# The last product of the down projection ended in two halves of its tokens, and residual sums made by accumulating transfers

## The chip, the core and the metric

The kernel runs on one core of one Trainium2 chip. The metric is the device time of one execution in microseconds (us); the figure for a kernel is the median of its runs. One execution of the kernel was recorded by the hardware profiler, instruction by instruction. The engines are named as in the profile: PE multiplies matrices, PEld is its loading of weights, DVE and ACT work element by element, POOL and SP here mostly issue transfers (DMAs). Tiles are 128 partitions high; matmul results go to PSUM banks of 128 x 512 floats, everything else lies in SBUF.

## What is computed

One layer of a decoder trunk, 1024 tokens of width 1024 in float32: a token-mixing part (an RWKV-7 branch and an S5 branch, merged) and then a channel part, each with a norm before and after and a residual sum:

```python
        mixed = (g_rwkv * o_rwkv + g_s5 * o_s5) @ w_out[l]
        x = x + rms_norm(mixed, norm_mix_post[l])
        h = rms_norm(x, norm_ffn_pre[l])
        f = conv_ffn(h, ffn_w_up[l], ffn_conv_w[l], ffn_conv_b[l], ffn_w_down[l])
        x = x + rms_norm(f, norm_ffn_post[l])

def conv_ffn(h, w_up, conv_w, conv_b, w_down):
    L = h.shape[1]
    z = h @ w_up
    zp = jnp.pad(z, ((0, 0), (CONV_WIDTH - 1, 0), (0, 0)))
    z = conv_b + sum(conv_w[j] * zp[:, j:j + L] for j in range(CONV_WIDTH))
    gate, val = jnp.split(z, 2, axis=-1)
    return (jax.nn.gelu(gate) * val) @ w_down
```

`rms_norm` divides each token by the root of the mean of its squares over the 1024 channels and scales each channel by a gain. The change is in the last two lines of the layer: the product with `w_down` (2816 by 1024), its norm, and the residual sum that is the output.

## The kernel before

Channels lie on partitions and tokens along the free dimension, so the layer's output is eight blocks of 128 channels by 1024 tokens. Every float32 matmul is done as three: an operand is split into a rounded high part (ACT, line 227) and the rest (DVE, line 228), and high x high, high x low and low x high are summed.

Four stages follow each other: the mixing part, its output projection with the norms between the two parts (`mid_norms`), the up stage (`fast_up`), and the down stage (`down`). `mid_norms` calls `post_norm`, which stores the residual stream x after the mixing part to a DRAM array `X1`, one block of 128 channels and 512 tokens at a time.

**The up stage** makes, for each of 22 tiles of the hidden width, a value and a gate, convolves both over the tokens in tiles `y` (one activation at line 1356, two DVE steps at line 1358 each), applies Gelu to the gate (line 1290), multiplies (line 1291) and has POOL store the result to the DRAM array `ACT[i]` (line 1292). Its tiles lie in four pools, one above the other in each partition: `upz` (bytes 25920 to 46400), `ups` (to 66880), `upr` (the weights as they arrive, `r`, and one split tile; to 83264) and `upy` (three buffers for `y`; to 95552).

**The down stage** multiplies two-by-two blocks of the product in seven block products instead of eight, by sums and differences of blocks; each covers 11 tiles of 128 of the hidden width. The products run in the order p1, p2, p5, p6, p7, p4, p3. Each takes its 11 tiles in six groups (`DGROUPS`: two, two, one, two, two, two tiles). For a group, `operands` splits both sides into `wh`, `wl`, `xh`, `xl`, in a ring of three sets; `step` issues three matmuls of 512 columns (lines 1511 to 1513) for one tile and one of four output banks `d`. In the first and the last group the banks are done one after the other, in the others the tiles are. `p1` loads a group's A and T tiles, which stay in SBUF, and its right operand into a ring of four staging tiles `st`, and takes the difference of T and `st` on DVE (line 1466). Its pools on the lower side are `dqa` (S, B and `sq` tiles; bytes 25920 to 66880), `dqs` (the `st` ring; 66880 to 83264) and `dqb` (B tiles; to 95552): they lie where the up stage's pools lay.

The norm and the output of the first 512 tokens are done between the groups of p3 (`middle`): after group 0 the squares are summed over the channels by matmuls with a column of ones (line 246) and DVE makes the reciprocal root (`rstd`, lines 266 and 136 to 141, a chain of 12 small instructions); after group 1 matmuls with the identity spread it over the partitions (`spread`, line 272); after group 3 `outputs` makes eight blocks on DVE, each a product with gain and root (line 1555) and a sum with the residual (line 1463), which SP stores to the output. The residual blocks were loaded from `X1` by `resid`, into freed T tiles. The other 512 tokens go the same way after p3's last group, their residual loaded into freed A tiles: `c12` adds each finished bank to its partial sum and ACT squares it (line 1537).

The order of work on each engine is made by a scheduler from the order in which the kernel is written, priorities and estimated times, and each queue runs strictly in its order. A tile in a pool that lies over an earlier pool may be written only when the users of the earlier pool are done.

Of the kernel before, what the change touches and what calls it, by code (L numbers as in the profile page):

```python
# [18 lines left out]
D = 1024  # L19
# [52 lines left out]
class Kern:  # L72
# [169 lines left out]

    def sumsq(self, ss, sq, first):

        for tb in range(4):
            self.nc.tensor.matmul(ss[:, tb:tb + 1], sq[:, tb * 128:(tb + 1) * 128], self.ones1,
                                  start=first and tb == 0, stop=True, skip_group_check=True)
# [14 lines left out]

    def rstd(self, ss, eps, scale):

        v = self.small.tile([128, 4], F32, tag="rv", name=self.nm("rv"), bufs=2)
        self.nc.vector.tensor_scalar(v, ss[:, :4], scale, eps, ALU.mult, ALU.add)
        return self.rsqrt(v, 4, "nr")

    def spread(self, bc, y):

        for tb in range(4):
            self.nc.tensor.matmul(bc[:, tb * 128:(tb + 1) * 128], y[:, tb:tb + 1].to_broadcast([128, 128]),
                                  self.cst("ident"), start=tb == 0, stop=True, skip_group_check=True)
# [950 lines left out]
    def mid_norms(self, th, mx):  # L1224
# [7 lines left out]
        yield from self.post_norm(mx, s0, th, "g_mix_post", lambda k, o: self.a["x"][k * 128:k * 128 + 128, o],  # L1232
                                  lambda k, o: self.X1[k * 128:k * 128 + 128, o], squares=ss)
        y = self.rstd(ss, 1e-6, 1.0 / D)
# [180 lines left out]
    def down(self, dq0, dqf, dqt, dqa, dqs, dqb):  # L1415
# [91 lines left out]

        def step(op, q, m, ps, start, stop):
            (wh, wl), (xh, xl) = op
            c, x = slice(q * 512 + m * 128, q * 512 + m * 128 + 128), slice(q * 512, q * 512 + 512)  # L1510
            mm(ps, wh[:, c], xh[:, x], start=start, stop=False, skip_group_check=True)  # L1511
            mm(ps, wh[:, c], xl[:, x], start=False, stop=False, skip_group_check=True)  # L1512
            mm(ps, wl[:, c], xh[:, x], start=False, stop=stop, skip_group_check=True)  # L1513
# [3 lines left out]

        def product(prep, ps, first, evict, between=lambda g: None):

            for g in range(ng):  # L1520
# [20 lines left out]

        def resid(th):
            xs = []
            for m in range(0, NK, 2):
                t = cache("T" if th == 0 else "A", (0, 1, 3, 4)[m // 2])
                for q in range(2):
                    x = t[:, q * 512:q * 512 + 512]
                    nc.sync.dma_start(x, self.X1[(m + q) * 128:(m + q) * 128 + 128, th * 512:th * 512 + 512])
                    xs.append(x)
            return xs  # L1550

        def outputs(th, src, bc, xs):
            for m in OUTORD[th]:
                y = stage(0)[:, 0:512]
                V.scalar_tensor_tensor(y, src[m], self.vec("g_ffn_post", m), bc, ALU.mult, ALU.mult)
                add(y, y, xs[m])
                nc.sync.dma_start(self.out[m * 128:m * 128 + 128, th * 512:th * 512 + 512], y)
        acc = [None, None]
# [25 lines left out]

        def c12(m):
            add(f[1][m], f[1][m], x[m])
            if m < 3:
                squares(1, f[1][m])
            else:
                last.append(acc[1])  # L1590
                acc[1] = None
                squares(1, f[1][m])

        def middle(g):
            if g == 0:
                ss = bank(0)
                self.sumsq(ss, acc[0], True)
                d["y"] = self.rstd(ss, 1e-6, 1.0 / D)
                d["xs"] = resid(0)
            elif g == 1:  # L1600
# [3 lines left out]
                A.copy(d["bc"], bc)  # L1604
            elif g == 3:
                outputs(0, f[0], d["bc"], d["xs"])
                d["xs1"] = resid(1)
        d, last = {}, []
        product(p1, b, True, keep1)
# [4 lines left out]
        product(p4, b, False, c21)  # L1614
        product(p3, x, False, c12, middle)
        ss = bank(2)
        self.sumsq(ss, last[0], True)
        self.sumsq(ss, acc[1], False)
        y = self.rstd(ss, 1e-6, 1.0 / D)
        bc = bank(3)  # L1620
        self.spread(bc, y)
        outputs(1, f[1], bc, d["xs1"])

    def build(self):
        tc, nc = self.tc, self.nc
        with tc.tile_pool(name="const", bufs=1) as self.const, tc.tile_pool(name="small", bufs=1) as self.small, \
# [10 lines left out]
            self.YR = [dr(f"YR{m}") for m in range(4)]  # L1637
            self.X1 = dr("X1", (D, T))
            self.H0 = [dr(f"H0{k}", (128, 512)) for k in range(NK)]
# [174 lines left out]
DGROUPS = ((0, 1), (2, 3), (10,), (4, 5), (6, 7), (8, 9))  # L1814
OUTORD = ((0, 1, 2, 3, 4, 5, 6, 7), (4, 5, 6, 7, 0, 1, 2, 3))
NT2C = 7
# [73 lines left out]
```

## Time and profile before

| | us |
|---|---|
| median of 3 runs | 1600.54 |
| lowest and highest run | 1599.51, 1603.78 |
| the profiled execution, as timed | 1601.3 |
| its span, first to last instruction | 1599.5 |
| PE busy within the span | 1501.5 (94%) |
| DVE busy | 1130.4 (71%) |
| ACT busy | 694.0 (43%) |
| POOL busy | 154.9 (10%) |

A row of the timeline gives the start from the span's beginning, the length, the engine, the line of the kernel, the operation, the tiles written and read, the shape and the count of rows merged; in brackets stand the idle time of the engine before it and what ended that. SPq is the issue of a transfer on SP's queue. A row of groups gives the count, the busy time, the mean in ns of one instruction and the idle time before them. A row of windows gives a stretch, its length, the busy time of PE, PEld, DVE, ACT and POOL with their instructions, the clock granted to PE as a share, the share of the DMA engines' time in use and GB/s. A row of DMA issues gives the tiles, the queue, the count, the size of one and the median time from issue to landing.

### The profile page before, as it was taken

The numbers are of one execution on the slowest core, as the hardware profiler recorded it, in microseconds if no ns is written. First come the engines' busy times: TensorE is split into PE (matmuls) and PEld (weight loads), VectorE is DVE, ScalarE is ACT, GpSimd is POOL, SyncE is SP. The second block draws the span as 40 slices with busy tenths as digits, with TensorE's granted clock in tenths as the row PEclk, the third lists the DMA queues.
The fourth block names the chain that finished last, engine by engine and source line by source line (L and its number), as shares of the span: only waits on it lengthen the run. The fifth ranks groups of instructions, "written<-read, shape, count | busy, mean of one in ns | idle before, by whom it ended". The sixth has DMA issues, their size and how long they took to land.

```text
span 1599.5 us, 26116 instructions
## 1 busy us (share of the span) xinstructions
PE 1501.5 (94%) x10028; PEld 1203.0 (75%) x10028; DVE 1130.4 (71%) x2039; ACT 694.0 (43%) x1107; POOL 154.9 (10%) x226
## 2 busy tenths in 40 slices
PE   5999899899999989979997999999999999999995
PEld 4788788687666766657776888788888887878784
DVE  6798774655365557874667679877777777688777
ACT  5354442224333345454533545544544445443451
POOL 2100000414123142010000000000000000000000
PEclk9999999999998989989988999999999999999997
DMA  6164244343352364652484453322222225953722
GB/s 205 40 198 142 72 128 138 104 129 120 101 151 84 104 192 119 180 146 68 152 259 142 145 191 130 122 91 79 79 80 92 80 79 166 325 186 116 226 80 105
DMA packets 133420, 213.84 MB, mean 134 GB/s; under 512 B 38656, under 2 KB 44800, under 8 KB 133296
## 3 DMA queue, kind: packets, MB, share of 16 engines
q1 hardware_dynamic: 124208, 188.32, 36.2%
q0 software_dynamic: 7936, 21.77, 4.6%
q10 hardware_dynamic: 1152, 2.10, 0.3%
q8 instruction: 78, 1.28, 0.3%
q14 instruction: 46, 0.38, 0.1%
HBM read 156.56 MB, written 53.48 MB: 131 GB/s over the span
## 4 chain that ended last, share of the span: by engine, by line
PE 57%; DVE 8%; DMA 3%; issue 1%; ACT 1%; POOL 0%; SPq 0%; DVEq 0%; ACTq 0%
PE gm L173 4%; PE rp L1337 4%; PE rp L1339 4%; PE rp L1338 4%; PE d L1512 4%; PE d L1511 4%; PE d L1513 4%; PE gm L174 3%; PE gm L175 3%; PE ch L173 2%; PE mm L1338 2%; PE mm L1337 2%; PE mm L1339 2%; PE ch L174 2%; PE ch L175 2%; PE mm L173 2%
## 5 line engine op out<-in xcount | busy, mean ns | idle before, releaser
L173 PE MATMUL gm<-hh,wh 128*128 128x512 f32 x688 | 297.3, 432 | 7.3 <-ACT hh L227 2.1
L174 PE MATMUL gm<-hl,wh 128*128 128x512 f32 x688 | 275.1, 400 | 0.4 <-DVE hl L228 0.4
L175 PE MATMUL gm<-hh,wl 128*128 128x512 f32 x656 | 261.4, 398 | 0.0
L157 ACT CAST wh<-wf 128x512 fp32r<-128x512 f32 x179 | 110.9, 619 | 219.7 <-PE gm L174 133.5
L158 DVE TENSOR_TENSOR wl<-wf,wh 128x512 fp32r<-128x512 f32 x175 | 121.9, 697 | 103.4 <-ACT wh L157 83.1
L173 PEld LDWEIGHTS gm<-hh,wh 128*128 128x128 f32 x688 | 132.5, 193 | 46.0 <-issue 5.1
L174 PEld LDWEIGHTS gm<-hl,wh 128*128 128x128 f32 x688 | 132.8, 193 | 24.3 <-issue 1.9
L175 PEld LDWEIGHTS gm<-hh,wl 128*128 128x128 f32 x656 | 126.2, 192 | 28.6
L1511 PE MATMUL d<-xh,wh 128*128 128x512 f32 x308 | 121.6, 395 | 2.8 <-ACT xh L227 2.1
L1512 PE MATMUL d<-xl,wh 128*128 128x512 f32 x308 | 121.5, 394 | 2.9 <-DVE xl L228 2.9
L1513 PE MATMUL d<-xh,wl 128*128 128x512 f32 x308 | 121.1, 393 | 0.0
L1337 PE MATMUL rp<-t,h 128*128 128x512 f32 x216 | 84.4, 391 | 2.1 <-ACT p L1351 2.1
L1339 PE MATMUL rp<-t,l 128*128 128x512 f32 x216 | 84.2, 390 | 0.5 <-DVE l L228 0.5
L1338 PE MATMUL rp<-t,h 128*128 128x512 f32 x216 | 84.1, 389 | 0.0
L1511 PEld LDWEIGHTS d<-xh,wh 128*128 128x128 f32 x308 | 58.5, 190 | 16.2 <-ACT xh L227 2.5
L1512 PEld LDWEIGHTS d<-xl,wh 128*128 128x128 f32 x308 | 58.6, 190 | 15.8 <-DVE xl L228 3.7
L1513 PEld LDWEIGHTS d<-xh,wl 128*128 128x128 f32 x308 | 58.7, 191 | 12.2
L228 DVE TENSOR_TENSOR l<-r,h 128x1024 fp32r<-128x1024 f32 x34 | 41.6, 1225 | 29.4 <-ACT h L227 27.8
L227 ACT CAST h<-r 128x1024 fp32r<-128x1024 f32 x34 | 35.9, 1054 | 61.1 <-PE rp L1338 32.5
L1358 DVE SCALAR_TENSOR_TENSOR y<-zv,vecs,y 128x1023 f32<-128x1023 f32 (+1 forms) x36 | 46.1, 1281 | 8.5 <-ACT y L1356 8.5
L1337 PEld LDWEIGHTS rp<-t,h 128*128 128x128 f32 x216 | 40.5, 188 | 11.6 <-ACT p L1351 2.9
L1339 PEld LDWEIGHTS rp<-t,l 128*128 128x128 f32 x216 | 40.5, 188 | 9.4 <-DVE l L228 1.0
(441 smaller groups left out, 3385.6 us busy)
## 6 DMA issues: line engine op xcount, KB each, us to landing
r<-in_w_up_dram SPq DMA_DIRECT2D x36, 512.0 KB, 3.3
wf<-in_w_in_dram SPq DMA_DIRECT2D x68, 256.0 KB, 2.7
st<-in_w_down_dram SPq DMA_DIRECT2D x55, 256.0 KB, 4.3
st<-ACT SPq DMA_DIRECT2D x44, 256.0 KB, 4.7
wf<-in_w_up_dram SPq DMA_DIRECT2D x36, 256.0 KB, 2.8
ACT<-y POOLq DMA_DIRECT2D x18, 512.0 KB, 2.9
GT<-ev SPq DMA_DIRECT2D x32, 256.0 KB, 2.2
wf<-in_w_br_dram SPq DMA_DIRECT2D x32, 256.0 KB, 2.9
```

Source lines behind the costliest of these rows:

```text
L157: nc.scalar.copy(h[:, :n], f[:, :n])
L158: nc.vector.tensor_tensor(l[:, :n], f[:, :n], h[:, :n].bitcast(F32), ALU.subtract)
L173: mm(ps, a, xh[k], start=k == 0, stop=False)
L174: mm(ps, a, xl[k], start=False, stop=False)
L175: mm(ps, b, xh[k], start=False, stop=k == n - 1)
L1337: mm(ps, wh[:, c], xh, start=first and k == 0, stop=False, skip_group_check=True)
L1338: mm(ps, wh[:, c], xl, start=False, stop=False, skip_group_check=True)
L1339: mm(ps, wl[:, c], xh, start=False, stop=k == 3, skip_group_check=True)
L1358: V.scalar_tensor_tensor(y[:, lag:], z[:, 0:1024 - lag], self.vec(nme, i), y[:, lag:], ALU.mult, ALU.add)
L1511: mm(ps, wh[:, c], xh[:, x], start=start, stop=False, skip_group_check=True)
L1512: mm(ps, wh[:, c], xl[:, x], start=False, stop=False, skip_group_check=True)
L1513: mm(ps, wl[:, c], xh[:, x], start=False, stop=stop, skip_group_check=True)
```

## The change

The residual stream after the mixing part is stored into the output array itself, and `X1` is gone. The outputs of the first 512 tokens are made in place by one DVE product each and added to the output array by a transfer that accumulates, issued by POOL; they load no residual. p3 runs its first three groups as before. The last three (24, 24 and 24 matmuls of 512 columns) are then run twice with 256 columns, first for one half of the second 512 tokens, then for the other (`halves`). The first half's sums of squares and root (`normed`) are issued behind the second half's first group, its spread and outputs (`shown`) behind the second group. Of the eight output blocks of a half, four (first half) and two (second half) are added by accumulating transfers; the others are added on DVE to residual tiles loaded from the output array and stored by SP. In each half the squares of the fourth bank are not added to the others' sum but go to PE as a second tile. The squares' tiles `sh` (four of 128 x 256) are new in pool `dqa`, and `small` gets six new tiles for the root.

```diff
-    def sumsq(self, ss, sq, first):
-        for tb in range(4):
+    def sumsq(self, ss, sq, first, n=4):
+        for tb in range(n):
...
-                                  lambda k, o: self.X1[k * 128:k * 128 + 128, o], squares=ss)
+                                  lambda k, o: self.out[k * 128:k * 128 + 128, o], squares=ss)
...
-        def step(op, q, m, ps, start, stop):
+        def step(op, q, m, ps, start, stop, cols=slice(0, 512)):
...
-            c, x = slice(q * 512 + m * 128, q * 512 + m * 128 + 128), slice(q * 512, q * 512 + 512)
+            c, x = slice(q * 512 + m * 128, q * 512 + m * 128 + 128), slice(q * 512 + cols.start, q * 512 + cols.stop)
...
-        def resid(th):
-            xs = []
-            for m in range(0, NK, 2):
-                t = cache("T" if th == 0 else "A", (0, 1, 3, 4)[m // 2])
+        def block(m, c):
+            return self.out[m * 128:m * 128 + 128, c]
+
+        def resid():
+            xs = [None] * NK
+            for n in range(4):
+                t = cache("A", (0, 1, 3, 4)[n])
                 for q in range(2):
-                    x = t[:, q * 512:q * 512 + 512]
-                    nc.sync.dma_start(x, self.X1[(m + q) * 128:(m + q) * 128 + 128, th * 512:th * 512 + 512])
-                    xs.append(x)
+                    m = LATE[2 * n + q]
+                    xs[m] = t[:, q * 512:q * 512 + 512]
+                    nc.sync.dma_start(xs[m], block(m, slice(512, 1024)))
             return xs
 
-        def outputs(th, src, bc, xs):
-            for m in OUTORD[th]:
-                y = stage(0)[:, 0:512]
-                V.scalar_tensor_tensor(y, src[m], self.vec("g_ffn_post", m), bc, ALU.mult, ALU.mult)
-                add(y, y, xs[m])
-                nc.sync.dma_start(self.out[m * 128:m * 128 + 128, th * 512:th * 512 + 512], y)
+        def output(y, m, c, bc, x):
+            V.scalar_tensor_tensor(y, y, self.vec("g_ffn_post", m), bc, ALU.mult, ALU.mult)
+            if x is None:
+                nc.gpsimd.dma_start(block(m, c), y, accum_op=ALU.add)
+            else:
+                add(y, y, x)
+                nc.sync.dma_start(block(m, c), y)
...
-                d["xs"] = resid(0)
             elif g == 1:
                 bc = bank(1)
                 self.spread(bc, d["y"])
                 d["bc"] = dq0.tile([128, 512], F32, tag="bc", name=self.nm("bc"), bufs=1)
                 A.copy(d["bc"], bc)
-            elif g == 3:
-                outputs(0, f[0], d["bc"], d["xs"])
-                d["xs1"] = resid(1)
+                d["xs"] = resid()
+
+        def halves():
+
+            ops = [p3(g) for g in range(3, ng)]
+            for m in range(NK):
+                output(f[0][m], m, slice(0, 512), d["bc"], None)
+            for h in range(2):
+                cols = slice(256 * h, 256 * h + 256)
+                ready = []
+                for n, op in enumerate(ops):
+                    qm = [(q, m) for q in range(2) for m in range(4)]
+                    if n == 2:
+                        qm = [(q, m) for m in range(4) for q in range(2)]
+                    for q, m in qm:
+                        step(op, q, m, x[m][:, cols], False, n == 2 and q == 1, cols)
+                        if n == 2 and q == 1:
+                            y = f[1][m][:, cols]
+                            add(y, y, x[m][:, cols])
+                            sq = dqa.tile([128, 256], F32, tag="sh", name=self.nm("sh"), bufs=4)
+                            A.activation(sq, y, AF.Square)
+                            if m < 3:
+                                add(sq, sq, ready[-1] if ready else acc[1][:, cols])
+                            ready.append(sq)
+                    if h and n == 0:
+                        normed(0, d["sq"])
+                    elif h and n == 1:
+                        shown(0)
+                d["sq"] = ready[2:]
+            normed(1, d["sq"])
+            shown(1)
+
+        def normed(h, sq):
+            ss = bank(2 - 2 * h)
+            for n in range(2):
+                self.sumsq(ss, sq[n], n == 0, 2)
+            d["y"] = self.rstd(ss, 1e-6, 1.0 / D, 2)
+
+        def shown(h):
+            bc = bank(3 - 2 * h)
+            self.spread(bc, d["y"], 2)
+            cols = slice(256 * h, 256 * h + 256)
+            for n, m in enumerate((4, 5, 6, 7, 0, 1, 2, 3)):
+                output(f[1][m][:, cols], m, slice(512 + 256 * h, 768 + 256 * h), bc[:, 0:256],
+                       None if n < (2 if h else 4) else d["xs"][m][:, cols])
...
-        product(p3, x, False, c12, middle)
-        ss = bank(2)
-        self.sumsq(ss, last[0], True)
-        self.sumsq(ss, acc[1], False)
-        y = self.rstd(ss, 1e-6, 1.0 / D)
-        bc = bank(3)
-        self.spread(bc, y)
-        outputs(1, f[1], bc, d["xs1"])
+        product(p3, x, False, None, middle, 3)
+        halves()
```

More of the change, by code (lines that the diff above doesn't have):

```diff
@@ L261, in square_into, with rstd, spread @@
         return sq
[L263 to L271, printed above, removed]
+    def rstd(self, ss, eps, scale, n=4):
+        v = self.small.tile([128, n], F32, tag=f"rv{n}", name=self.nm("rv"), bufs=2)
+        self.nc.vector.tensor_scalar(v, ss[:, :n], scale, eps, ALU.mult, ALU.add)
+        return self.rsqrt(v, n, f"nr{n}")
+    def spread(self, bc, y, n=4):
+        for tb in range(n):
             self.nc.tensor.matmul(bc[:, tb * 128:(tb + 1) * 128], y[:, tb:tb + 1].to_broadcast([128, 128]),
@@ L1516, in bank, with product @@
             return self.ps.tile([128, 512], F32, tag=f"d{m}", name=self.nm("d"), bufs=1)
-        def product(prep, ps, first, evict, between=lambda g: None):
-            for g in range(ng):
+        def product(prep, ps, first, evict, between=lambda g: None, end=None):
+            for g in range(end or ng):
                 op = prep(g)
@@ L1583, in c21 @@
             squares(1, f[1][4 + m])
[L1585 to L1592, printed above, removed]
         def middle(g):
@@ L1604, in middle @@
                 A.copy(d["bc"], bc)
-            elif g == 3:
-                outputs(0, f[0], d["bc"], d["xs"])
-                d["xs1"] = resid(1)
-        d, last = {}, []
+                d["xs"] = resid()
[39 more added lines that the diff above has]
+                       None if n < (2 if h else 4) else d["xs"][m][:, cols])
+        d = {}
         product(p1, b, True, keep1)
@@ L1637, in build @@
             self.YR = [dr(f"YR{m}") for m in range(4)]
-            self.X1 = dr("X1", (D, T))
             self.H0 = [dr(f"H0{k}", (128, 512)) for k in range(NK)]
@@ L1814 @@
 DGROUPS = ((0, 1), (2, 3), (10,), (4, 5), (6, 7), (8, 9))
-OUTORD = ((0, 1, 2, 3, 4, 5, 6, 7), (4, 5, 6, 7, 0, 1, 2, 3))
+LATE = (4, 5, 6, 7, 0, 1, 2, 3)
 NT2C = 7
```

## The prediction

> **What bounds the kernel now.** I read the page first, then the windows of the last 25 us, then the timeline of each engine there, then the change of stage into the down projection.
>
> ```profile
> span 1599.5 us, 26116 instructions
> PE 1501.5 (94%) x10028; PEld 1203.0 (75%) x10028; DVE 1130.4 (71%) x2039; ACT 694.0 (43%) x1107; POOL 154.9 (10%) x226
> 1575.00:1590.00 15.00, 7.10 (x38) 5.88 (x36) 9.88 (x25) 2.17 (x4) 0.00 (x0) 0.70 0.08 30
> 1590.00:1600.00 10.00, 0.00 (x0) 0.00 (x0) 6.12 (x10) 0.00 (x0) 0.00 (x0) 0.50 0.43 165
> ```
>
> PE sets the pace, so an idle PE is lost time unless it is made up. The windows (PE, PEld, DVE, ACT, POOL, clock, DMA share, GB/s) show the part the change aims at: after 1577.8 PE has almost nothing to do and one chain runs alone.
>
> ```profile
> 1577.58 0.39 PE L1513 MATMUL d<-xh,wl 128*128 128x512 f32 x1
> 1579.35 2.06 PE L246 MATMUL d<-ones,sq 128*128 128x1 f32 x16 [1.38 <-DVE sq L1463]
> 1581.45 0.16 DVE L266 TENSOR_SCALAR rv<-d 128x4 f32<-128x4 f32 x1 [2.15 <-PE d L246]
> 1583.84 2.08 PE L272 MATMUL d<-csts,rsy 128*128 128x128 f32 x8 [2.43 <-DVE rsy L141]
> 1585.95 1.41 DVE L1555 SCALAR_TENSOR_TENSOR st<-r,vecs,d 128x512 f32<-128x512 f32 x2 [2.17 <-PE d L272]
> 1587.27 1.29 DVE L1463 TENSOR_TENSOR st<-st,A 128x512 f32<-128x512 f32 x2
> 1594.83 1.29 DVE L1463 TENSOR_TENSOR st<-st,A 128x512 f32<-128x512 f32 x2
> 1561.98 34.51 SPq L1557 DMA_DIRECT2D out_dram<-st  x16
> ```
>
> Each line waits for the one above it: the squares summed on PE 2.1, the reciprocal root on DVE 2.4 (1581.45 to 1583.84), its spread over the partitions 2.1, sixteen DVE instructions 10.2 (1585.95 to 1594.83 + 1.29 = 1596.12), the last store and its landing 3.4 to 1599.5. SP has sixteen output stores in this stretch, eight for each half of the sequence.
>
> **What the built order adds.** The trace of before cannot show what the change does to the order and the waits of the other stages; the two built programs can. They differ in one place outside the tail, where the up stage hands over to the down stage. The first load of p1's right operand, which p1's first matmul needs, waits for:
>
> ```
> before  st<-ACT0  [waits DMAHW2_49,DMASW3_49,DVE_49]
> after   st<-ACT0  [waits DMASW4_49,DMASW5_49,DMASW3_49,DMASW6_49,DMASW2_49,DMASW7_49,DMASW1_49,DMAHW5_49,DMASW0_49,DVE_49]
> ```
>
> In the built programs the four new `sh` tiles (4 KB) lie in `dqa`, below `dqs`. Before, `dqs` (the `st` ring) covered bytes 66880 to 83264, exactly pool `upr` of the up stage; now it covers 71168 to 87552 and reaches into `upy` (83456 to 95744), the output tiles `y`. A tile whose pool lies over an earlier pool waits for the last user of that pool, not only of its own bytes: the DMASW4 count in the second row is reached by the last store of the up stage, ACT[21]<-y, and by no earlier one. SP's order has changed with it: after A come all eleven T loads, four A, four S, and only then the seven `st` loads of p1's first four groups.
>
> ```profile
> 1344.07 3.17 SPq L1442 DMA_DIRECT2D st<-ACT  x7
> 1348.12 1.06 ACT L227 CAST xh<-st 128x1024 fp32r<-128x1024 f32 x1 [2.92 <-DMA st<-ACT]
> 1353.70 3.23 SPq L1442 DMA_DIRECT2D T<-ACT  x7
> 1356.00 0.39 PE L1339 MATMUL mm<-hh,w 128*128 128x512 f32 x1
> 1358.45 0.47 PE L1511 MATMUL d<-xh,wh 128*128 128x512 f32 x1 [2.06 <-ACT xh L227]
> 1358.75 0.40 PE L1512 MATMUL d<-xl,wh 128*128 128x512 f32 x1
> 1358.34 1.25 ACT L1356 ACTIVATE y<-zg,vecs 128x1024 f32<-128x1024 f32 x1
> 1359.41 1.22 DVE L1466 TENSOR_TENSOR T<-T,st 128x1024 f32<-128x1024 f32 x1
> 1360.55 1.28 DVE L1358 SCALAR_TENSOR_TENSOR y<-zg,vecs,y 128x1023 f32<-128x1023 f32 x1
> 1361.74 1.22 DVE L228 TENSOR_TENSOR xl<-st,xh 128x1024 fp32r<-128x1024 f32 x1
> 1366.51 1.06 ACT L1290 ACTIVATE y<-y 128x1024 f32<-128x1024 f32 x1
> 1367.60 1.23 DVE L1291 TENSOR_TENSOR y<-y,y 128x1024 f32<-128x1024 f32 x1 [1.70 <-ACT y L1290]
> 1369.12 0.53 POOL L1292 DMA_DIRECT2D ACT<-y  x1 [16.72 <-DVE y L1291]
> ACT<-y POOLq DMA_DIRECT2D x18, 512.0 KB, 2.9
> ACT<-y POOLq DMA_DIRECT2D x1, 512.0 KB, 5.1
> ```
>
> Before, `st` was requested 12 us before the up stage's last matmul, and p1 began at 1358.45, while that stage's last gated tile was still in work; its store went out at 1369.12, beside p1.
>
> **Part 1, the held start (cost).** In before's times: the gate's first activation still starts at 1358.34 and ends at 1359.6. p1's T subtraction and xl no longer stand between, so two convolution steps of about 1.2, Gelu 1.06 and the product 1.23 follow: 1364.6; the store goes out 0.3 later, 1364.9. It lands 2.9 (all eighteen) to 5.1 later (the last one, in the loaded stretch). I take 4.5, near the loaded row, since T, A and S loads fill the queues then: 1369.4. SP then issues `st`: 1344.07 to 1348.12 is 4.05 from issue to cast, so 1373.45. On DVE the T subtraction is now ahead of xl (about 1.2 each): p1's second matmul at 1375.85 against 1358.75. **+17.1 us**, nothing covers it: PE's order is unchanged, and p1 to p3 all stand behind p1's first matmul. Bounds: 2.9 for the landing gives 15.5; 5.1 and a slower `st` (+1) give 18.7. Queued behind SP's wait are the later loads of p1 and p2, and behind DVE's T subtraction the other splits of p1. T, A and the first S are already in, and each group of two tiles has 24 matmuls of 0.227 (the rows are below), 5.4 us, to fetch and split the next one under: two loads, a subtraction and a split of 1.2 each. I cost them nothing; what would end that cover is a DMA queue that falls behind, and it has 15 loads less to do from there.
>
> ```profile
> 1360.00:1362.00 2.00, 2.00 (x6) 1.54 (x6) 2.00 (x3) 0.00 (x0) 0.00 (x0) 0.50 0.99 368
> 1420.93 0.47 PE L1511 MATMUL d<-xh,wh 128*128 128x512 f32 x1 [0.78 <-DVE p L1463]
> 1502.45 0.74 PE L1512 MATMUL d<-xl,wh 128*128 128x512 f32 x1 [1.95 <-DVE xl L228]
> ```
>
> The clock after the pause is no new cost: a 2.06 us pause already brought it to 0.50. What a late start could win back is only what PE loses later: 0.78, 1.95, and, by the row above with six matmuls in 2 us where nine fit, under 2 of slow clock behind the latter: 4.5 at most. Both pauses are put down to DVE, whose order there is unchanged, so I take 0.
>
> **Part 2, p3's end (gain).**
>
> ```profile
> 1550.21 0.94 PE L246 MATMUL d<-ones,sq 128*128 128x1 f32 x8
> 1551.02 0.49 PE L1511 MATMUL d<-xh,wh 128*128 128x512 f32 x1
> 1559.93 1.41 DVE L1555 SCALAR_TENSOR_TENSOR st<-p,vecs,bc 128x512 f32<-128x512 f32 x2
> 1560.25 0.39 PE L1511 MATMUL d<-xh,wh 128*128 128x512 f32 x1
> 1571.13 0.39 PE L1511 MATMUL d<-xh,wh 128*128 128x512 f32 x1
> 1570.05 1.22 DVE L228 TENSOR_TENSOR wl<-S,wh 128x1024 fp32r<-128x1024 f32 x1
> 1571.19 1.22 DVE L228 TENSOR_TENSOR xl<-B,xh 128x1024 fp32r<-128x1024 f32 x1
> 1572.46 0.50 PE L1512 MATMUL d<-xl,wh 128*128 128x512 f32 x1 [0.94 <-DVE xl L228]
> L1513 PEld LDWEIGHTS d<-xh,wl 128*128 128x128 f32 x308 | 58.7, 191 | 12.2
> ```
>
> The halves begin where group 3 began, 1560.25. A 512-column matmul takes 0.227 (48 in 10.88). 256 columns are not in the trace: half is 0.113, and eight 1-column matmuls, each with its weights, took 0.81, 0.101 each. I take 0.12, nearest to the half; bounds 0.101 and 0.19 (a weight load's own 191 ns, if nothing of it overlapped: the halves load every weight twice, 144 loads for 72). DVE at 256 columns, an estimate by the slope between 512 and 1024 columns (a sum 0.61 and, 1570.05 to 1571.19, 1.14; a scaled product 0.66, and 1.28 against 0.75 for one alone): 0.34 for a sum, 0.39 for a product.
>
> The first 512 tokens' eight sums and their SP stores go. Before, group 5's split (1570.05) stood behind all sixteen of their instructions; now it stands behind three products, is done by 1564.4, and the 0.94 stall goes; next late is nothing, since PE needs it at 1566. 72 matmuls of 0.12: half 0 ends at 1568.9. Half 1 writes the other columns of the same banks, and each bank's first matmul waits for DVE's eviction of half 0 there; DVE is free at 1567.6 and is ahead of it. Half 1's group 3 (2.9), the sums (8 of 0.1), group 4 (2.9, which covers the 2.4 of the root), the spread and its way to DVE (0.6): 1576.1. DVE then does half 0's eight products and four sums, 4.5, to 1580.6, while PE finishes group 5 at 1578.8. The evictions of half 1 stand behind these outputs on DVE, though their banks are ready: seven instructions of 0.34, 1583.1. Sums 1.05 (half of 2.1), rsqrt 2.4, spread 1.05: 1587.6. Eight products and six sums: 5.3, so 1593 against 1596.12, and a 128 KB last store some 0.2 sooner. **-3.3 us.** Bounds: with 0.101 the spread comes 2 us sooner and DVE with it, -5.3; with 0.19 half 0 ends at 1573.9 and half 1 (13.7 and 1.2 of small matmuls) at 1588.8, and a last eviction, sums, root, spread and outputs of 10.7 end at 1599.5, +3.4.
>
> The Trainium skill, TensorE: Matmul & The Clock Gate, LDWEIGHTS (loading the stationary operand), puts a load of 128 columns at columns over 1.2 GHz, 107 ns. By it 256 columns sit just at the load's limit and the halves would cost 0.11 each, 1.4 us less on PE; the 0.101 here agrees with it.
>
> **Part 3, accumulating transfers.** No such transfer is in the trace. Fourteen on POOL's queue, eight of 256 KB from 1562 on and six of 128 KB; the last is issued at about 1588.5, 7 us before the last plain store lands. The nearest rows are POOL's 512 KB stores, 2.9 to 5.1: hidden, 0. They would have to take over 7 us, or queue at over 3.4 us each, to set the end. The Trainium skill, SBUF — State Buffer, SBUF: two separate sides, says that a transfer issued by GpSimd cannot get its descriptors while DVE runs a two-port operation. By it, if these products and sums are such operations, the last two could start only after DVE's end at 1593 and, at 2.9 to 5.1, end up to 1.5 us past my end; the eighteen stores, 2.9 in the middle beside a DVE that is busy 71%, do not show it.
>
> **Sum.** 1601.3 (the profiled run: span 1599.5 and 1.8 around it) + 17.1 - 3.3 = 1615.1; that run stood 0.8 above the median of 1600.54, so **1614.3**.
>
> **Rivals.** Slack: PE's later stalls vanish, as DMA runs ahead after the pause: 1614.3 - 4.5 = 1609.8; for it, the two rows above, against it, DVE and not DMA released both. Weight loads: 256-column matmuls take 0.19: 6.7 more, 1621; against it the 0.101. Accumulation slow: at 5 each in turn, the eight end at 1602 and the six of half size at 1617 in before's times, 21 later than the plain end: 1635. The other side: **the hold does not bind**, because the last gated tile is stored before p1 would need `st`; then only the tail counts: 1600.5 - 3.3 = 1597. It decides if the store landed by about 1354, and that tile's last matmul is at 1356. That the change does nothing (the end merely moves from DVE to the stores): 1600.5.
>
> **Numbers.** Forecast 0.72, slack 0.08, weight loads 0.08, slow accumulation 0.05, no hold 0.05, nothing 0.02. Two kernels here can be told apart from 0.3%, 4.8 us. Slower 0.93, same 0.02, faster 0.05. Range: 1614.3 less 1.6 (landing) and 4.5 (slack) to plus 1.6 and 6.7 is 1608 to 1622, with 0.10 outside by the cases and some for what I have overlooked.
>
> **What would show it.** Right: the first d matmul some 16 us later behind an idle PE, ACT's xh waiting for DMA st, SP's wait on that landing; S and T loads ahead of `st`. At the end about 15 us from the last big matmul to DVE's end, DVE between half 0's outputs and half 1's evictions without a pause. Wrong: PE idle by 2 to 3 us only at the first d matmul, or a pitch of 0.19 in the halves, or the end set by POOL's queue.

## The result, and the profile after

The changed kernel is slower, as forecast, but by more: 1625.2 us (median of four runs, 1623.96 to 1625.8) against 1602.2 for the kernel before, run on the same chip (1599.51 to 1604.61). The ratio is 1.0143, 95% interval 1.0123 to 1.0163: 23 us more (19.7 to 26.1) where 13.8 were forecast. The profiled execution took 1625.8.

```profile
span 1623.7 us, 26277 instructions
PE 1509.1 (93%) x10100; PEld 1208.2 (74%) x10100; DVE 1128.5 (70%) x2060; ACT 695.1 (43%) x1111; POOL 168.6 (10%) x240
```

The timeline of the hand-over from the up stage to the down stage, after:

```profile
1362.32 0.39 PE L1339 MATMUL mm<-hh,w 128*128 128x512 f32 x1
1369.00 1.06 ACT L1290 ACTIVATE y<-y 128x1024 f32<-128x1024 f32 x1 [3.13 <-DVE y L1358]
1370.01 2.26 SPq L1436 DMA_DIRECT2D S<-in_w_down_dram  x4
1370.09 1.23 DVE L1291 TENSOR_TENSOR y<-y,y 128x1024 f32<-128x1024 f32 x1 [1.18 <-ACT y L1290]
1371.61 0.53 POOL L1292 DMA_DIRECT2D ACT<-y  x1 [13.54 <-DVE y L1291]
1378.37 3.17 SPq L1442 DMA_DIRECT2D st<-ACT  x7
1382.33 1.04 ACT L227 CAST xh<-st 128x1024 fp32r<-128x1024 f32 x1 [12.27 <-DMA st<-ACT]
1383.42 0.80 PE L1511 MATMUL d<-xh,wh 128*128 128x512 f32 x1 [20.71 <-ACT xh L227]
1384.76 0.79 PE L1512 MATMUL d<-xl,wh 128*128 128x512 f32 x1 [0.54 <-DVE xl L228]
```

The chain is the forecast one: the last gated tile, its store (1371.61), only then the first load of `st` (1378.37), the cast, the first `d` matmul behind 20.71 us of idle PE where there were 2.06. The last up matmul, however, is itself at 1362.32 and not at 1356.00.

The end, after; first the timeline of PE and DVE, and SP's last issue:

```profile
1576.27 0.95 PE L246 MATMUL d<-ones,sq 128*128 128x1 f32 x8
1586.26 0.28 PE L1511 MATMUL d<-xh,wh 128*128 128x256 f32 x1
1597.78 0.95 PE L246 MATMUL d<-ones,sh 128*128 128x1 f32 x8
1602.18 1.66 DVE L1556 SCALAR_TENSOR_TENSOR r<-r,vecs,d 128x256 f32<-128x256 f32 x4 [1.09 <-PE d L272]
1606.66 1.08 DVE L1463 TENSOR_TENSOR q<-q,d 128x256 f32<-128x256 f32 x3
1609.63 1.83 PE L246 MATMUL d<-ones,sh 128*128 128x1 f32 x8 [4.62 <-DVE sh L1463]
1613.98 1.20 PE L272 MATMUL d<-csts,rsy 128*128 128x128 f32 x4 [2.51 <-DVE rsy L141]
1615.21 1.66 DVE L1556 SCALAR_TENSOR_TENSOR r<-r,vecs,d 128x256 f32<-128x256 f32 x4 [1.38 <-PE d L272]
1618.69 2.28 SPq L1561 DMA_DIRECT2D out_dram<-q  x4
1619.69 0.75 DVE L1463 TENSOR_TENSOR q<-q,A 128x256 f32<-128x256 f32 x2
```

With these rows and those of before, the 24.2 us between the two spans fall into four stretches:

| stretch | before | after | difference |
|---|---|---|---|
| start to last up matmul | 1356.00 | 1362.32 | +6.3 |
| from there to p1's second matmul | 2.75 | 22.44 | +19.7 |
| from there to the column sums of the first norm | 191.46 | 191.51 | 0.0 |
| from there to the end of the span | 49.3 | 47.4 | -1.9 |

The second row is the held start, the fourth the halves. The first had no term in the prediction. The 0.0 of the third belongs to these two executions alone: over the executions of all kernels below, that stretch takes 187.9 to 191.5 us. The windows of PE in the steady part of the up stage show where some of it went: before, then after.

```profile
1100.00:1300.00 200.00, 200.00 (x884) 1.00 0.22 82
```

```profile
1100.00:1300.00 200.00, 200.00 (x877) 1.00 0.22 82
```

PE is busy throughout, at full clock (1.00), and yet gets through seven matmuls fewer in 200 us: 228.1 ns from the start of one to the start of the next (the pitch) in place of 226.2. The groups of the same window, before:

```profile
L1338 PE MATMUL rp<-t,h 128*128 128x512 f32 x127 | 49.4, 389 | 0.0
```

and after:

```profile
L1338 PE MATMUL rp<-t,h 128*128 128x512 f32 x126 | 49.6, 394 | 0.0
L1337 PE MATMUL rp<-t,h 128*128 128x512 f32 x126 | 49.4, 392 | 0.0
L1339 PE MATMUL rp<-t,l 128*128 128x512 f32 x126 | 48.9, 388 | 0.0
L1337 PE MATMUL mm<-hh,w 128*128 128x512 f32 x40 | 15.6, 389 | 0.0
```

The same instruction in the same order takes 394 ns in place of 389 (this length counts a part that overlaps the next matmul); with the weights `w` nothing has changed (the row of `w` above stands in before's view word for word). What sets the groups apart is where the weights lie. The six new tiles of the pool `small` moved all pools of the lower side by 192 bytes, with them the weight tiles `h`, `l`; `w` and the activations `hh`, `hl`, `t` lie in pools of the other side and did not move.

### The profile page after: what moved, and what is told of

It reads as the page before. It is cut to its first block, busy times and chain, and to the rows that moved or that the text cites. A ratio compares the mean times of both kernels' runs of the same rounds, so it can differ in the third digit from the quotient of the medians.

```text
span 1623.7 us, 26277 instructions
## 1 busy us (share of the span) xinstructions
PE 1509.1 (93%) x10100; PEld 1208.2 (74%) x10100; DVE 1128.5 (70%) x2060; ACT 695.1 (43%) x1111; POOL 168.6 (10%) x240
## 4 chain that ended last, share of the span: by engine, by line
PE 63%; issue 17%; DVE 11%; DMA 4%; POOL 2%; ACT 2%; SPq 0%; POOLq 0%; DVEq 0%; ACTq 0%
PE gm L173 9%; PE gm L174 7%; PE gm L175 7%; PE d L1512 4%; PE d L1513 4%; PE d L1511 4%; PE ch L173 2%; PE ch L174 2%; PE ch L175 2%; PE mm L173 2%; PE mm L174 2%; PE mm L175 2%; PE rp L1337 2%; PE rp L1338 2%; PE rp L1339 2%
## 5 line engine op out<-in xcount | busy, mean ns | idle before, releaser
L1511 PE MATMUL d<-xh,wh 128*128 128x512 f32 (+1 forms) x332 | 126.3, 380 | 20.7 <-ACT xh L227 20.7
L1512 PE MATMUL d<-xl,wh 128*128 128x512 f32 (+1 forms) x332 | 126.1, 380 | 2.8 <-DVE xl L228 2.8
L1513 PE MATMUL d<-xh,wl 128*128 128x512 f32 (+1 forms) x332 | 125.7, 379 | 0.0
L1511 PEld LDWEIGHTS d<-xh,wh 128*128 128x128 f32 x332 | 63.6, 192 | 32.7 <-ACT xh L227 21.1
L1512 PEld LDWEIGHTS d<-xl,wh 128*128 128x128 f32 x332 | 63.5, 191 | 15.0 <-DVE xl L228 3.7
L1513 PEld LDWEIGHTS d<-xh,wl 128*128 128x128 f32 x332 | 63.5, 191 | 11.4
```

## The experiments

Each ratio is against runs of the kernel before on the same chip.

| kernel | what it is | ratio | 95% interval |
|---|---|---|---|
| e1_small_back | changed, 192 bytes taken back | 1.0106 | 1.0071 to 1.0141 |
| e2_ring_back | changed, ring over its old pool | 1.0007 | 0.9989 to 1.0025 |
| e3_both_back | both | 0.9990 | 0.9968 to 1.0013 |
| e4_before_shifted | before, moved by 192 bytes | 1.0019 | 1.0000 to 1.0037 |
| e7_ring_64 | before, ring 64 bytes up | 1.0127 | 1.0100 to 1.0153 |
| e9_both_sides | e4, other side moved too | 0.9980 | 0.9963 to 0.9998 |
| e12_both_sides_again | e9 again | 0.9972 | 0.9954 to 0.9989 |
| e6_vector_adds | e3, no accumulating transfer | 1.0054 | 1.0034 to 1.0075 |
| e10_undivided | e3, end undivided | 1.0002 | 0.9986 to 1.0019 |
| e5_order | e3, DVE's order changed | 0.9968 | 0.9948 to 0.9988 |
| e11_order_both_sides | e5 with e9's places | 0.9955 | 0.9937 to 0.9973 |

### The two causes, each taken back

My theory after the result: two placements in SBUF cost the time, the 192 bytes (a slower triple, the three matmuls that make up one product) and the ring's reach (the held start); the end in halves itself gains. Rivals: the early loss comes from storing the residual stream in the output array; the start is held by SP's longer queue of loads.

e1, the norm's small tiles as slices of the old ones:

```diff
...
-        v = self.small.tile([128, n], F32, tag=f"rv{n}", name=self.nm("rv"), bufs=2)
+        v = self.small.tile([128, 4], F32, tag="rv", name=self.nm("rv"), bufs=2)[:, :n]
...
```

> The changed kernel, with one thing taken back: the half norms use slices of the four-column tiles that the other norms use, so the pool of small tiles has its old 2,432 bytes a partition and no pool behind it moves by 192 bytes. The ring of staging tiles still reaches 4 KB further than before. Address theory (the 7 us that the changed kernel has lost by the end of the up stage come from the 192 bytes, by which the weight tiles h1, l1 and h2, l2 moved against the activations hh and hl; the triple of matmuls took 0.680 us before and 0.687 after): the triple is back at 0.680, the last up matmul ends near 1356, and the time is 1625.2 - 7 = 1618. Storage theory (they come from x + mix being written to the output's rows in place of a buffer of its own): nothing changes, 1625.

e2, the squares' tiles in the last pool:

```diff
-                            sq = dqa.tile([128, 256], F32, tag="sh", name=self.nm("sh"), bufs=4)
+                            sq = dqb.tile([128, 256], F32, tag="sh", name=self.nm("sh"), bufs=4)
```

> The changed kernel, with the four half-square tiles in the last pool (dqb) in place of dqa, so that the staging ring lies exactly over the pool upr again and not over a part of upy; the pools still lie 192 bytes further up. Theory of the held start (the first staging load waits for the last activation store, since its tile reaches into a tile y): the load goes out some 19 us earlier, the second down matmul comes 0.3 us after the first as before, and the time is 1625.2 - 19 = 1606, with the last up matmul still near 1362.6. Rival (the loads are late for another reason, as the longer queue of loads on SyncE or a slower store): the second down matmul stays some 20 us behind the last up matmul, 1625.

e3 has both edits at once:

> The changed kernel with both of the edits beside this: half norms in slices of the old small tiles, half squares in the last pool. What is left of the change is the end in halves, the accumulating transfers and the residuals from the output. If the two causes are all that made it slower and add up, 1625.2 - 7 - 19 = 1599, which is 3 under the 1602.2 of the kernel before; by the gain of the end as the traces have it (1.8 us) 1600.4. If the earlier 7 us come from the storage of x + mix, 1606. If something else holds the start, 1618 or more.

e4 is the kernel before with one line more:

```diff
+                self.nc.gpsimd.memset(self.small.tile([128, 42], F32, name="shift"), 0.0)
```

> The kernel before, with one unused tile of 168 bytes a partition in the pool of small tiles, so that all pools behind it lie 192 bytes further up; the staging ring still lies exactly over upr. Address theory: triples of the up stage at 0.687 in place of 0.680, hand-over 7 us later, 1602.2 + 7 = 1609. Storage theory, or any other cause in the end of the kernel: 1602, no difference.

The windows of PE over the same 200 us, e3 and then e4:

```profile
1100.00:1300.00 200.00, 200.00 (x884) 1.00 0.25 85
```

```profile
1100.00:1300.00 200.00, 200.00 (x877) 1.00 0.25 85
```

e4 has nothing of the change but 192 bytes, and has its 877; e3 has all of the change but the two placements, and has 884. The storage theory falls. e2's first `st` load is out before the up stage ends, and its second down matmul comes as before:

```profile
1351.99 3.17 SPq L1442 DMA_DIRECT2D st<-ACT  x7
```

In the times, the places are worth +0.19% (e4) or, from e3 to e2, +0.17%: 3 us, but neither is clear of the noise (e4's interval begins at 1.0000, and those of e2 and e3 overlap). The held start is worth +1.27% (e7, below) or, from e3 to e1, +1.16%: 19 to 20 us. e1's 1.0106 fits the 1.010 of the address theory (1618 over 1602.2) and leaves the 1.0143 of the storage theory just outside its interval; the full 7 us that the address theory gave e4 are outside too. Halves and transfers together: -0.10% (e3), no difference that these runs can tell from none. The three add up to 1.0136 by e7, e4 and e3, against 1.0143 measured for all at once.

One expectation missed: e1's last up matmul did not return to 1356, it was at 1365.0, and e3's at 1367.3 (e2's, expected near 1362.6, was at 1365.9). Up to the up stage the profiled executions scatter by more than the 192 bytes are worth, at equal order and equal places: e6, built with the same places, had it at 1352.2. So the 6.3 of the first row of the table are not all shown to be the places. From 937 to 1333 us, where nothing scatters, the lag of after behind before, matmul by matmul, grows from 3.9 to 6.9, while e3's stays at 9.1; the 3.0 of that stretch are the slower triple, the 3.9 ahead of it lie within the scatter.

### What the 192 bytes do

e8 is the triple by itself:

```diff
...
+                w = slice(128 * (k % 4) + 16 * i, 128 * (k % 4) + 16 * i + 128)
+                x = slice(16 * j, 16 * j + 512)
+                mm(o, wh[:, w], xh[:, x], start=k == 0, stop=False, skip_group_check=True)
+                mm(o, wh[:, w], xl[:, x], start=False, stop=False, skip_group_check=True)
+                mm(o, wl[:, w], xh[:, x], start=False, stop=k == n - 1, skip_group_check=True)
...
```

> No part of the layer: the matmul triple alone (wh x xh, wh x xl, wl x xh, 128x128 by 128x512), the weights' slices beginning 0, 64, ... 448 bytes behind a multiple of 512 (from one common base) and the activations' the same, 64 pairs of 8 triples each, nothing else running; PSUM tiles oa to oh name the weights' offset, xa to xh the activations'. Relative theory: pairs of equal offset have the shortest pitch (227 ns in the up stage before), others up to 232 or more, by the difference of the two. Absolute theory: the pitch depends on one of the two alone. Third: 227 for all, as the pitch needs other traffic in SBUF to differ.

Its timeline, cut to the first matmul of five pairs in a row; `b` in `xbh` is an activation offset of 64 bytes, `oa` to `oe` weight offsets of 0 to 256:

```profile
74.86 0.39 PE L1895 MATMUL oa<-xbh,wh 128*128 128x512 f32 x1
...
80.37 0.40 PE L1895 MATMUL ob<-xbh,wh 128*128 128x512 f32 x1
...
85.83 0.40 PE L1895 MATMUL oc<-xbh,wh 128*128 128x512 f32 x1
...
91.43 0.39 PE L1895 MATMUL od<-xbh,wh 128*128 128x512 f32 x1
...
97.00 0.39 PE L1895 MATMUL oe<-xbh,wh 128*128 128x512 f32 x1
```

24 matmuls each: 5.51 us with the activations 64 bytes ahead of the weights, 5.46 at equal offset, 5.60 and 5.57 at 64 and 128 behind. Within the pairs, the mean distance from start to start (each pair's two longest left out) depends on one number, (activation offset - weight offset) modulo 256, in all 64 pairs:

| difference modulo 256, bytes | 0 | 64 | 128 | 192 |
|---|---|---|---|---|
| ns from start to start | 226.7 | 229.0 | 231.5 | 233.0 |

The values of one column agree within 0.4 ns, but for one pair of equal offset at 227.7. Neither offset alone matters, and no other engine has to be at work: in the whole stretch of pairs (28 to 384 us) DVE makes one copy of 0.69 us and ACT and POOL nothing, at clock 1.00. Why the distance counts is not shown. By the built addresses, in the kernel before both sides lay 64 bytes behind a multiple of 256; the 192 bytes put the weights at 0 and made the difference 64. If so, moving the other side too must cure it, as e9 does:

```diff
-                self.nc.gpsimd.memset(pad.tile([128, 40], F32, name="pad"), 0.0)
+                self.nc.gpsimd.memset(pad.tile([128, 120], F32, name="pad"), 0.0)
+                self.nc.gpsimd.memset(self.small.tile([128, 42], F32, name="shift"), 0.0)
```

> e4_before_shifted (the kernel before, left pools 192 bytes up), with the pad on the right side 320 bytes larger, so that weights and activations both begin at a multiple of 512 bytes; in the kernel before both begin 320 bytes behind one. Relative theory: the triple of the up stage is back at 0.680 us and the time is that of before. Absolute theory: it stays at 0.687 or becomes longer still, 0.2% over before or more.

Its PE window:

```profile
1100.00:1300.00 200.00, 200.00 (x884) 1.00 0.22 82
```

The pitch is back. The time went further than expected, below that of before. e12 is the same kernel again, to see whether the place itself is worth something.

> e9_both_sides once more, in more rounds on another chip. Difference alone counts: 1.000 of the kernel before. The place itself is worth something: 0.998 again.

It came out at 0.9972, below 1 as well. The up stage takes 345.6 (e9) and 345.5 us (e12) from its first to its last matmul, 346.2 before; but e7, whose weights lie as before, has 345.6 too. Most of what the two profiles win lies between p1's second matmul and the first norm, 189.1 and 187.9 us in place of 191.5, and that stretch scatters at the old places too (e3 188.1, e10 190.2). This gain is measured twice and not explained.

### What the ring waits for

> The kernel before, with one unused tile of 64 bytes a partition in the pool ahead of the staging ring: the ring lies 64 bytes further up and so reaches 64 bytes into the pool upy, by its highest tile alone; nothing else of the kernel differs, and all weights lie where they lay. Theory of the held start, whole pools (the first load of the ring waits for the release of every pool under the ring): the first load goes out some 16 us behind the last up matmul in place of 12 ahead of it, the first down matmul 21 us behind it in place of 2.4, 1.012 of the time before. By tiles (a load waits for what lies under its own tile): the first load goes out as before, the second (whose tile is the highest) waits; the first down matmul comes at 2.4, and the stall behind it is shorter. By bytes (64 of them cost in proportion): no difference.

```diff
+        dqa.tile([128, 16], F32, tag="gap", name=self.nm("gap"), bufs=1)
         acc = [None, None]
```

The timeline of e7 at the hand-over:

```profile
1363.83 0.39 PE L1339 MATMUL mm<-hh,w 128*128 128x512 f32 x1
...
1373.13 0.53 POOL L1292 DMA_DIRECT2D ACT<-y  x1 [13.38 <-DVE y L1291]
...
1379.86 3.17 SPq L1442 DMA_DIRECT2D st<-ACT  x7
...
1385.15 0.80 PE L1511 MATMUL d<-xh,wh 128*128 128x512 f32 x1 [20.93 <-ACT xh L227]
```

64 bytes cost the price of the 4 KB (+19.7 us in the table above, +1.16% from e3 to e1): the first load 16.0 us behind the last up matmul, 1.0127 of the time before. The wait is for whole pools; by tiles the first load, whose tile lies at the ring's low end, would have gone out as before.

### Where the end's gain comes from

e6 loads all residuals and adds them on DVE:

```diff
...
-                output(f[0][m], m, slice(0, 512), d["bc"], None)
+                output(f[0][m], m, slice(0, 512), d["bc"], d["xs0"][m])
...
```

> As e3_both_back, but every residual is loaded and added by VectorE, none by an accumulating transfer: eight more loads of 256 KB, eight more additions of 128x512 (0.67 us each) in the first half of the end, four of 128x256 (0.38 us) ahead of the second half's evictions and two in the last outputs. If the accumulating transfers are hidden, as predicted, they save those additions and nothing is lost by them: this one is slower by 4 x 0.38 + 2 x 0.38 = 2.3 us at least, and by up to 7 where the first eight additions push the evictions back. If the accumulating transfers held up the end (their queue moved 150 to 200 GB/s with the DMA engines over 0.9 busy), this one is faster.

```profile
1568.97 0.58 PE L1511 MATMUL d<-xh,wh 128*128 128x256 f32 x1 [3.74 <-DVE q L1463]
```

From the first norm's column sums to the end it took 55.6 us, 8.5 more than e3: above the expected 7. In its PE timeline (the row above) the second half's first matmul waits 3.74 us for DVE, which evicts the first half's banks (adds them to their partial sums) only after the first 512 tokens' sums. With this order on DVE the accumulating transfers are not just hidden; the halves need them.

e10 keeps them and undoes the halves (one run of 512 columns, four accumulated outputs at the end):

```diff
-            for h in range(2):
-                cols = slice(256 * h, 256 * h + 256)
...
+                    step(op, q, m, x[m], False, n == 2 and q == 1)
...
+                output(f[1][m], m, slice(512, 1024), bc, None if n < 4 else d["xs"][m])
```

> As e3_both_back, but with the end of the last product undivided (512 columns, all four evictions, one norm), the residuals of the first half of the tokens and of four of the last eight outputs still by accumulating transfers. From the column sums of the first norm to the end the kernel before took 49.3 us, e3_both_back 47.1. If the gain comes from the additions that the transfers take over: 49.3 - 4 x 0.68 = 46.6, as good as the halves or better. If it comes from the halves, because the first one's norm and outputs lie beside the second's matmuls: 49 or more, since the last accumulating transfers of 256 KB land some 9 us behind their issue.

Its last rows on DVE and on SP:

```profile
1594.20 4.08 SPq L1561 DMA_DIRECT2D out_dram<-q  x4
1595.97 1.29 DVE L1463 TENSOR_TENSOR q<-q,A 128x512 f32<-128x512 f32 x2
```

and from its DMA issues:

```profile
out_dram<-r POOLq DMA_DIRECT2D x4, 256.0 KB, 5.9
out_dram<-q SPq DMA_DIRECT2D x4, 256.0 KB, 5.8
```

Neither forecast holds. DVE's end comes 3.7 us nearer to the first norm (42.2 against 45.9), but the last plain stores, 256 KB beside accumulating ones, take 5.8 us to land (2.1 in before, where nothing accumulates), and the end comes only 0.9 nearer (48.4 against 49.3). e3, with outputs of 128 KB, has 47.1. So the halves and the transfers both have a share in these traces; the times of e3 and e10 cannot be told apart.

e5 changes the order on DVE, where the trace of after shows 4.5 us of first-half outputs (1602.18 to 1606.66) ahead of evictions whose banks were ready:

```diff
-                        shown(0)
+                        bc0 = spread(0)
+                        shown(0, bc0, (4, 5))
...
-            normed(1, d["sq"])
-            shown(1)
+            ss = sums(1, d["sq"])
+            shown(0, bc0, (0, 1, 2, 3))
+            with self.tc.manual_schedule(engines={mybir.EngineType.DVE}):
+                root(ss)
+                bc1 = spread(1)
+                shown(0, bc0, (6, 7))
+                shown(1, bc1, range(NK))
```

> The changed kernel with both pools back (as in e3_both_back), and VectorE's order in the last stretch changed: of the first half's eight outputs only two come before the second half's evictions and squares, four while TensorE sums the squares, two while it spreads the norm. In e3_both_back the eight outputs took 4.5 us ahead of the second half's first eviction (1588.56, where its matmuls ended near 1586.9), and VectorE then stood idle for 2.0 and 1.4 us in the norm. Theory of the end (VectorE's order sets it): the column sums start 3 us earlier against the last matmul and the whole is 2.9 us under e3_both_back, 0.998 of it and some 0.996 to 0.997 of the kernel before. Rival (the end is set by the outputs' transfers): no difference to e3_both_back.

Its timeline: evictions, column sums, root.

```profile
1585.27 1.12 DVE L1463 TENSOR_TENSOR q<-q,d 128x256 f32<-128x256 f32 x3
1588.31 1.55 PE L246 MATMUL d<-ones,sh 128*128 128x1 f32 x8 [1.67 <-DVE sh L1463]
1589.90 0.16 DVE L266 TENSOR_SCALAR rv<-d 128x2 f32<-128x2 f32 x1 [0.56 <-PE d L246]
```

PE's idle time ahead of the column sums falls from 4.62 to 1.67, DVE's ahead of the root from 2.02 to 0.56, and the end comes 44.8 us behind the first norm's sums, 2.3 nearer than in e3. The ratio, 0.9968, is the expected one, though its interval still overlaps that of e3. e11 is e5 with e9's places:

> e5_order with the bases of e9_both_sides (weights and activations both at a multiple of 512 bytes, in place of 320 behind one). If only the difference of the two places counts, as the 64 pairs have it, the time is that of e5_order, 0.997 of the kernel before. If the place itself is worth the 0.2% by which e9_both_sides came out below the kernel before (0.998, 0.9963 to 0.9998), 0.995.

0.9955 is the lowest ratio of all, with medians of 1596.39 against 1601.99 us. Its interval holds both forecasts, 0.995 and 0.997, and overlaps that of e5, so it does not settle whether the place itself is worth something.

## Why the prediction was right or wrong

**The held start: right in mechanism and place, one term too small.** The store went out 9.3 us behind the last up matmul where the prediction's times make 8.9; `st` took 3.96 from issue to cast where 4.05 was taken. The step that failed is the landing of the last store: taken at 4.5, between 2.9 and 5.1, it was 6.8 from its issue to SP's next (1371.61 to 1378.37; 6.4 of it the landing); e7 has 6.7. The sum is 19.7 in place of 17.1, above the upper bound of 18.7. Windows beside the last store, before and then after, and two rows of DMA issues of after show what else the queues did meanwhile:

```profile
1369.00:1374.00 5.00, 5.00 (x24) 4.14 (x23) 5.00 (x6) 2.29 (x3) 0.53 (x1) 1.00 0.96 344
1369.00:1378.00 9.00, 0.00 (x0) 0.00 (x0) 1.23 (x1) 1.06 (x1) 0.53 (x1) 0.50 0.96 344
```

```profile
S<-in_w_down_dram SPq DMA_DIRECT2D x4, 256.0 KB, 5.7
ACT<-y POOLq DMA_DIRECT2D x1, 512.0 KB, 6.4
```

The DMA engines are as full (0.96) beside either store. What differs is how many loads were still under way at the store's issue: by the issues and landings in the traces five before, eight after. Over the profiles of all kernels here the last up-stage store landed in 4.2 to 5.5 us with four or five loads ahead of it and in 6.1 to 6.8 with seven or eight (e3, whose start is not held, has 6.8 with seven); the store before it, with at most three ahead, took 2.9 each time. The prediction named the T, A and S loads for its 4.5, and then kept a bound from a stretch where fewer were ahead. That these loads are the cause is read from the traces; no run took them away.

**Everything ahead of the hand-over unchanged: wrong, a term left out.** The prediction took it that the two programs "differ in one place outside the tail" and put nothing on the rest. Its own addresses show the 192 bytes (`upy` from 83264 to 83456). I asked only which pools now overlap, not what the addresses do to the matmuls. Runs put 3 us on it (e4: 0 to 5.9), the traces 3.0 from 937 to 1333 us.

**Slack won back: none that shows, as taken.** It took 191.46 and 191.51 us from p1's second matmul to the first norm. Executions of that stretch scatter by more than 3 us, but those with a held start (after, e1, e7) average 190.2 and the ten others 190.0.

**The end: right up to the last norm, then too short.** Counted from the halves' start (1560.25 and 1586.26), half 0's sums and spread and the end of its outputs (forecast 20.35, measured 20.40) came as predicted, and so did 0.12 us for 256 columns (96 matmuls in 11.52): the rival of slow weight loads is out. The evictions ended 0.4 late; then the sums took 1.83 where half of 2.06 was taken. That row came from PE at 0.84 clock after 1.38 us of idleness (the first window, of before); here PE had been idle for 4.62 (the second, of after):

```profile
1579.00:1582.00 3.00, 2.06 (x16) 1.97 (x16) 0.78 (x4) 0.36 (x1) 0.00 (x0) 0.84 0.01 3
1609.00:1612.00 3.00, 1.83 (x8) 1.78 (x8) 0.85 (x4) 0.00 (x0) 0.00 (x0) 0.50 0.31 89
```

The clock stood at 0.50. DVE's end came 1.4 us later than forecast, and the gain is 1.9 in these two profiles (2.3 as the mean of five profiles with the old end and four with the new one) in place of 3.3.

**The accumulating transfers: hidden, as forecast, though slow.** From the DMA issues of the last stretch of after:

```profile
out_dram<-p POOLq DMA_DIRECT2D x4, 256.0 KB, 5.8
out_dram<-s POOLq DMA_DIRECT2D x4, 256.0 KB, 9.1
out_dram<-r POOLq DMA_DIRECT2D x6, 128.0 KB, 4.2
```

The first eight were issued by 1595.7 and the last plain store sets the end. The Trainium skill's rule that a transfer issued by GpSimd waits for its descriptors beside a two-port operation of DVE (SBUF — State Buffer, SBUF: two separate sides) would have shown here in the last two, issued beside DVE's last products and sums, if these are such operations:

```profile
1615.99 1.76 POOL L1558 DMA_DIRECT2D out_dram<-r  x2 [9.49 <-DVE r L1556]
```

By the trace they landed at 1619.1 and 1620.9, the first ahead of DVE's end at 1620.4 and both ahead of the last plain store (1622.6), so this trace does not show it.

**The range.** Forecast +13.8 with up to +21.5 allowed. Landing (+2.3), store issue (+0.4), the moved weights (+3) and the end (+1.4) make up 7.1 of the missing 9. The rest is not assigned; it is not more than the interval of the ratio leaves open. No rival took the forecast's place.

## What to carry to other kernels

A tile added to any pool moves every pool behind it on its side, so ask two questions of the built addresses before any of the edit itself: which pools now lie over other pools (64 bytes over a boundary cost as much as 4 KB, 20 us here), and whether weights and activations still begin at the same place modulo 256 bytes. A tile that is only needed late belongs at the end of the last pool, or in a slice of one that exists. When a wait is priced, the landing that ends it is taken from a stretch with as many transfers ahead of it as the wait itself brings forward.

## What the runs showed of the hardware

A 512-column matmul (fp32r) was issued every 226.7 ns where its weights and activations begin at equal offsets modulo 256 bytes of a partition, and every 229.0, 231.5 or 233.0 ns at differences of 64, 128 or 192, with nothing else running (e8). A 256-column one was issued every 120 ns, weights loaded anew for each (after). By the median of each row of DMA issues (after, e3, e10), accumulating transfers to DRAM of 256 KB, four in a row, landed 4.8 to 9.3 us behind their issue, those of 128 KB 4.2 to 4.4; plain stores of 128 KB beside them took 2.9 to 3.5, of 256 KB 5.8, and of 256 KB without them 2.1 (before). A 512 KB store issued by POOL landed in 2.9 us with at most three loads of 256 KB under way and in 6.1 to 6.8 with seven or eight. Eight one-column matmuls took 0.95 us at full clock and 1.83 at 0.50 (after).
